# Encoder layer for two sequences: the split parts of ten weight chunks kept in DRAM by the first sequence and loaded by the second

## The chip, the core and the metric

One core of a Trainium2 chip runs the whole kernel in one launch. The metric is device time in microseconds (us); lower is better. TensorE (PE in the profile) does the matmuls, VectorE (DVE), ScalarE (ACT) and GpSimd (POOL) the rest; all transfers are issued by SyncE (SP), one after the other.

## What is computed

One encoder layer on two independent sequences of 512 rows with 1024 columns, float32 in and out. Cut to what matters here:

```python
h = rms_norm(x, pre_g)
z = h @ w_in                         # split into mixers, gates and merge gates
q = rms_norm(c_q, q_norm_g) @ w_uq   # 8 heads of 64 + 32 (rope) columns
kv = rms_norm(c_kv, kv_norm_g) @ w_ukv   # 8 heads: 64 columns of k, 64 of v
y_attn = attention(q, k, v) * silu(g_attn)
m = (gates[0] * (y_pool @ w_up_pool) + gates[1] * (y_attn @ w_up_attn)
     + gates[2] * (y_conv @ w_up_conv) + gates[3] * (y_four @ w_up_fourier))
out = x + rms_norm(m @ w_out, post_g)
```

Both sequences use the same weights: `w_uq` (chunks of kind h), the k and v columns of `w_ukv` (kinds kn and v) and the four `w_up` matrices (kind u) are the ones that count below.

## The kernel before

**Split matmuls.** A float32 operand is held as two fp32r parts, a rounded one (hi) and the rest (lo = source - hi). `mm3` (L569) makes a product of three matmuls: hi x hi, hi x lo, lo x hi. `split` (L574) makes the parts: an ACT copy writes hi, then a subtraction writes lo. The subtraction is recorded by `either`, so it may run on DVE or on POOL.

**Weight chunks.** A unit of work (`_Unit`) names the chunks that it needs by a key (sequence, kind, number). Line 619 sets the sequence to 0 for kinds that both sequences share, and for u chunks 0 to 5, which are used by both sequences in one stage; so these are loaded and split once. The chunks h 0 and 1 (128x768), kn 0 and 1 (128x256), v 0 and 1 (128x256) and u 6 to 9 (128x1024, the attention branch's up projection) carry the sequence's own number: they are loaded and split once for each sequence. `acquire` (L1632) does it: `load` (L1635) issues a DMA of the raw chunk, `into` (L1641) allocates the two parts and calls `split`.

**The order of the work.** Every call is recorded as an atom by `_Recorder`, and its `emit` (L182) writes all instructions, so nearly every row of the profile shows L182. `plan` (L285) is a list scheduler: it has one queue each for PE, ACT, DVE, POOL and the DMAs, prices for every operation (`price`, L184; a DMA costs `DMA_START` and its bytes over `DMA_RATE`, L113), due times that run back from PE's order, and a limit of buffers (42 of 2048 columns, 16 of 512). It picks at each step the atom that can start first, by due time, and for `either` the engine that would end first. What comes out is a fixed order for each engine. An instruction at the head of an engine's queue that waits holds all behind it. This is so for SP too: a DMA that stores a tile waits in SP's queue until the tile is written, and the DMAs behind it wait with it.

**The stages that matter.** After the group products of the input projection (until about 560 us) comes the tail, in which PE's order weaves two things: the up projections with their merges (u chunks), first the three branches that both sequences do together, then the attention branch of the first, then of the second sequence; and each sequence's attention. For a sequence, `c_units` (L745) fetches its projected rows cn from DRAM (four DMAs, `cn`, L756), mixes the rotated columns and transposes them on PE; `v_units`, `k_unit` and `q_unit` (L795 to L865) multiply them with v, kn and h chunks; each of the first two query blocks is put together by five or so DMAs from tile to tile (`b<-b` in the profile), the others are stored and fetched later. Then the heads follow.

Of the kernel before, what the change touches and what calls it, by code (L numbers as in the profile page):

```python
# [12 lines left out]
F32 = mybir.dt.float32  # L13
F32R = mybir.dt.float32r
# [4 lines left out]
P = 128  # L19
# [460 lines left out]
def trunk_kernel(ctx: ExitStack, tc: tile.TileContext, a: dict):  # L480
# [4 lines left out]
    rec = _Recorder()  # L485
# [9 lines left out]
    act, dve, pool, pe, sync = (Engine(e) for e in ("act", "dve", "pool", "pe", "dma"))  # L495

    def either(out, x, y, op):

        c = ("tensor_tensor", (out, x, y), dict(op=op))
        rec.choice(dve=c, pool=c)  # L500

    def copied(out, x):
        rec.choice(act=("activation", (out, x, AF.Copy), {}), dve=("tensor_copy", (out, x), {}))
# [6 lines left out]
    def g_(dt=F32, w=512):  # L510
        return rec.new("g", (P, w), dt)

    def b_(shape, dt=F32):
        return rec.new("b", [P] + list(shape), dt)

    def f_(w=D):
        return rec.new("f", (P, w), F32)
# [9 lines left out]
    def nm(s):  # L527
        uid[0] += 1
        return f"{s}_{uid[0]}"
# [14 lines left out]
    def stored(shape):  # L544
        n = nm("st")
        return rec.new("dram", shape, F32, dp.tile(list(shape), F32, tag=n, name=n))
# [27 lines left out]
    def split(hi, lo, src):  # L574
        act.activation(hi, src, AF.Copy)
        if src.buf.kind == "ps":
            dve.tensor_tensor(lo, src, hi.bitcast(F32), op=ALU.subtract)
        else:
            for c in ((slice(0, 1), slice(1, 2)) if lo.idx.ndim == 2 and lo.idx.size == D else (slice(None),)):
                either(lo[:, c], src[:, c], hi[:, c].bitcast(F32), ALU.subtract)  # L580
# [1051 lines left out]
    def acquire(key):  # L1632
        kind = key[1]

        def load(i):  # L1635
            src, w = srcs[i]
            r = f_(w)
            sync.dma_start(r, src)
            return r

        def into(src):  # L1641
            w = src.shape[1]
            t = b_([2, w], F32R) if w > 512 else rec.new("w" if w > 256 else "g", (P, 2, w), F32R)
            split(t[:, 0], t[:, 1], src)
            return t[:, 0], t[:, 1]
        if kind[0] == "l":
            m = R[LEFT[int(kind[1])]]
            return into(m[:, key[2], :])
        if kind in ("r1", "r2"):
            g = g_()  # L1650
            sync.dma_start(g, a["wo"][key[2] + 4 * (kind == "r2")][:, :512])
            return into(g)
        if kind == "r7":
            r1, r2 = [load(("o", key[2] + i)) for i in (0, 4)]
            s3 = g_()
            t1, t2, t4 = r1[:, :512], r1[:, 512:], r2[:, :512]
            either(s3, r2[:, 512:], t2, ALU.subtract)
            either(t1, t2, t1, ALU.subtract)
            either(t2, r2[:, 512:], t1, ALU.subtract)
            either(t4, t2, t4, ALU.subtract)  # L1660
            raws["o", key[2]] = {"r7": s3, "r5": t1, "r6": t2, "r4": t4, "r3": r2[:, 512:]}
        if kind[0] == "r":
            return into(raws["o", key[2]][kind])
        if key[1:] == ("q", 0):
            r, t = f_(832), b_([2, 832], F32R)
            for c in (slice(0, 416), slice(416, 832)):
                sync.dma_start(r[:, c], srcs["q", 0][0][:, c])
                copied(t[:, 0, c], r[:, c])
                dve.tensor_tensor(t[:, 1, c], r[:, c], t[:, 0, c].bitcast(F32), op=ALU.subtract)
            return t[:, 0], t[:, 1]  # L1670
        if kind == "q":
            r, t = load(key[1:]), b_([2, 832], F32R)
            copied(t[:, 0], r)
            either(t[:, 1], r, t[:, 0].bitcast(F32), ALU.subtract)
            return t[:, 0], t[:, 1]
        if kind[0] != "g":
            return into(load(key[1:]))
        if kind == "ga":
            r = raws[key[2]] = b_([2, 2, 512])
            for j, i in enumerate(PAIRS[key[2]]):  # L1680
                sync.dma_start(r[:, :, j, :], a["wt"][i].rearrange("p (h c) -> p h c", h=2))
            t = b_([2, 1024], F32R)
            split(*[t[:, i].rearrange("p (a b) -> p a b", a=2) for i in range(2)], r[:, :, 0, :])
            return t[:, 0], t[:, 1]
        r = raws[key[2]]
        r1a, r2a, r1b, r2b = [r[:, i, j, :] for i in range(2) for j in range(2)]
        if kind == "gb":
            s3 = raws["s3", key[2]] = g_()
            either(s3, r1a, r2a, ALU.subtract)
            either(r2a, r2a, r2b, ALU.add)  # L1690
            either(r1a, r2a, r1a, ALU.subtract)
        if kind == "gd":
            return into(raws["s3", key[2]])
        if kind == "gc":
            either(r1b, r1b, r1a, ALU.subtract)
        t = b_([2, 1024], F32R)
        split(*[t[:, i].rearrange("p (a b) -> p a b", a=2) for i in range(2)], r[:, int(kind == "gc")])
        return t[:, 0], t[:, 1]

    raws, owned = {}, set()  # L1700
    rec.unit()
    pool.memset(mhalf, -0.5)
    for n, u in enumerate(prog):
        if n == fixed:
            rec.floor = len(rec.segs)
        for k in u.chunks:
            if k not in owned:
                owned.add(k)
                rec.unit(0.0, None if n < fixed else PLAN["aheado" if k[1][0] in "lr" else "ahead"])
                live_chunks[k[1:]] = acquire(k)  # L1710
        rec.unit(u.cost, u.ahead if n >= fixed else None)
        u.fn()
# [124 lines left out]
```

## Time and profile before

| | us |
|---|---|
| median of 3 runs | 923.95 (922.61 to 928.17) |
| the profiled execution | 927.52 |
| its span on the core | 925.7 |
| PE busy | 898.8 (97%) |
| DVE, ACT, POOL busy | 721.9, 492.2, 359.4 |
| moved by DMA | 129.86 MB, 140 GB/s over the span |

The span runs from the first to the last record of the core; 1.8 us of the execution lie around it. The mean granted clock of TensorE was 0.997 of full speed. In the profile an operation is written as out<-in with the program's names, numbers left out: `ps` are PSUM tiles, `b` wide and `g` narrow SBUF tiles, `st` tiles in DRAM, `in_...` inputs in DRAM. "[0.5 <-DVE b]" behind a row says that the engine was idle for 0.5 us ahead of it, and that a DVE instruction on a `b` tile ended that.

### The profile page before, as it was taken

How to read it: one execution, taken by the hardware profiler on the slowest of the kernel's cores; microseconds unless marked ns; L12 is line 12 of the kernel's file. 1: busy time of each engine (PE TensorE's matmuls, PEld its weight loads, DVE VectorE, ACT ScalarE, POOL GpSimd, SP SyncE). 2: the span in 40 equal slices, each digit the busy share in tenths (PEclk: the TensorE clock that was granted, in tenths of full speed). 3: DMA queues.
4: the chain of work that ended last, by engine and by line, in shares of the span. 5: the costliest groups of instructions: out<-in, count | busy, mean ns of one | idle time of the engine just before them, and what ended most of it. 6: DMA issues, size and time to landing. Idle time of an engine off the chain costs nothing. (4 is left out here: it accounts for less than half of the span.)

```text
span 925.7 us, 12147 instructions
## 1 busy us (share of the span) xinstructions
PE 898.8 (97%) x4125; PEld 725.4 (78%) x4125; DVE 721.9 (78%) x1089; ACT 492.2 (53%) x871; POOL 359.4 (39%) x305
## 2 busy tenths in 40 slices
PE   7999999999999999999999999899999999999996
PEld 6897877888778888877888887787778777777784
DVE  6889999689994655667634367978899778899998
ACT  7964233345443345435444456855676678873253
POOL 2798432126331322346100031412353344246935
PEclk9999999999999999999999999999999999999998
DMA  7140123332232333543322447866754564461124
GB/s 273 64 152 10 58 103 125 129 110 103 91 125 106 128 133 130 173 142 118 136 104 102 141 141 179 254 217 198 233 186 133 161 242 148 155 231 58 37 101 182
DMA packets 62258, 129.86 MB, mean 140 GB/s; under 512 B 6890, under 2 KB 10483, under 8 KB 61684
## 3 DMA queue, kind: packets, MB, share of 16 engines
q1 hardware_dynamic: 62196, 129.09, 41.7%
q8 instruction: 32, 0.52, 0.2%
q14 instruction: 30, 0.25, 0.1%
HBM read 88.56 MB, written 37.36 MB: 136 GB/s over the span
## 5 line engine op out<-in xcount | busy, mean ns | idle before, releaser
L182 PE MATMUL ps<-b,b 128*128 128x512 f32 (+3 forms) x3428 | 808.1, 392 | 9.9 <-DVE b L182 4.7
L182 PEld LDWEIGHTS ps<-b,b 128*128 128x128 f32 (+1 forms) x3428 | 626.5, 187 | 158.0 <-DVE b L182 6.7
L182 ACT ACTIVATE b<-b 128x1024 fp32r<-128x1024 f32 (+9 forms) x164 | 141.3, 880 | 127.6 <-PE ps L182 46.4
L182 POOL TENSOR_TENSOR b<-b,b 128x512 fp32r<-128x512 f32 (+4 forms) x79 | 120.8, 1542 | 141.1 <-ACT b L182 134.5
L182 DVE TENSOR_TENSOR b<-b,b 128x512 fp32r<-128x512 f32 (+5 forms) x167 | 144.5, 892 | 31.6 <-ACT b L182 30.6
L182 POOL TENSOR_TENSOR b<-g,b 128x512 fp32r<-128x512 f32 x48 | 69.0, 1442 | 133.3 <-ACT b L182 133.3
L182 DVE TENSOR_TENSOR g<-ps,g 128x512 f32<-128x512 f32 (+4 forms) x101 | 66.2, 658 | 63.6 <-PE ps L182 35.8
L182 ACT ACTIVATE g<-ps 128x512 f32<-128x512 f32 (+5 forms) x110 | 59.4, 542 | 88.3 <-PE ps L182 71.9
L182 DVE TENSOR_TENSOR b<-ps,b 128x512 fp32r<-128x512 f32 (+2 forms) x128 | 85.0, 682 | 21.2 <-ACT b L182 20.4
L182 DVE SCALAR_TENSOR_TENSOR ps<-b,cols,ps 128x512 f32<-128x512 f32 x116 | 87.3, 752 | 2.7
L182 ACT ACTIVATE b<-g 128x512 fp32r<-128x512 f32 x101 | 61.5, 629 | 32.3 <-DVE g L182 18.5
L182 ACT ACTIVATE b<-ps 128x512 fp32r<-128x512 f32 (+2 forms) x116 | 66.5, 593 | 19.9 <-PE ps L182 19.2
L182 DVE TENSOR_TENSOR b<-b 128x512 f32<-128x512 f32 (+4 forms) x69 | 61.9, 898 | 9.0 <-POOL g L182 4.0
L182 ACT ACTIVATE g<-ps,s 128x512 f32<-128x512 f32 (+1 forms) x77 | 48.5, 639 | 23.8 <-DVE s L182 14.9
L182 ACT ACTIVATE g<-g,cols 128x512 f32<-128x512 f32 x48 | 34.6, 721 | 48.7 <-DVE g L182 48.3
L182 POOL TENSOR_TENSOR b<-b 128x512 f32<-128x512 f32 (+3 forms) x32 | 43.7, 1367 | 39.2 <-DVE b L182 16.2
L182 POOL TENSOR_TENSOR b<-b,g 128x512 f32<-128x512 f32 x26 | 37.2, 1436 | 51.1 <-DVE g L182 36.0
L182 DVE TENSOR_TENSOR b<-g,b 128x512 fp32r<-128x512 f32 x53 | 51.2, 980 | 4.6 <-ACT b L182 4.1
L182 PE MATMUL ps<-b 128*128 128x512 f32 (+1 forms) x216 | 52.1, 388 | 1.2 <-DVE b L182 1.2
L182 POOL TENSOR_TENSOR g<-b 128x512 f32<-128x512 f32 x15 | 20.1, 1342 | 80.5 <-DMA b<-in_wt 47.7
L182 DVE TENSOR_REDUCE s<-ps 128x1 f32<-128x512 f32 x64 | 43.4, 681 | 4.9 <-PE ps L182 4.5
L182 PEld LDWEIGHTS ps<-b 128*128 128x128 f32 x216 | 39.5, 188 | 9.7 <-issue 1.4
(74 smaller groups left out, 563.4 us busy)
## 6 DMA issues: line engine op xcount, KB each, us to landing
st<-g SPq DMA_DIRECT2D x104, 256.0 KB, 2.0
b<-in_wt SPq DMA_DIRECT2D x50, 512.0 KB, 4.7
g<-st SPq DMA_DIRECT2D x100, 256.0 KB, 3.4
b<-in_x SPq DMA_DIRECT2D x15, 512.0 KB, 4.5
b<-in_wup SPq DMA_DIRECT2D x14, 512.0 KB, 4.5
b<-st SPq DMA_DIRECT2D x4, 1024.0 KB, 6.8
b<-in_wo SPq DMA_DIRECT2D x8, 512.0 KB, 6.7
out_y<-b SPq DMA_DIRECT2D x16, 256.0 KB, 2.1
```

The lines of the kernel that those rows point to most:

```text
L182: getattr(engines[atom.eng], method)(*[real(x) for x in args], **{k: real(x) for k, x in kw.items()})
```

## The change

For the ten chunks h 0 and 1, kn 0 and 1, v 0 and 1 and u 6 to 9, the first sequence loads and splits as before and then issues two stores, of hi and of lo, to a DRAM tile of twice the chunk's width. The second sequence issues one load of that tile instead of the raw load, the ACT copy and the subtraction. `PLAN` and the prices are as they were; the scheduler makes a new order from the changed atoms. The number of PE instructions stays (4127 in the program); ACT has 13 fewer, DVE 11 fewer, POOL 4 more, SP 20 more.

```diff
@@ acquire
+        if kind in ("h", "kn", "v", "u") and key[0] + (kind == "u" and key[2] < 6) == 0:
+            got = into(load(key[1:]))
+            w = got[0].shape[1]
+            split_before[key[1:]] = stored((P, 2, w))
+            for i in range(2):
+                sync.dma_start(split_before[key[1:]][:, i, :], got[i].bitcast(F32))
+            return got
+        if key[1:] in split_before:
+            w = split_before[key[1:]].shape[2]
+            t = b_([2, w], F32R) if w > 512 else rec.new("w" if w > 256 else "g", (P, 2, w), F32R)
+            sync.dma_start(t.bitcast(F32), split_before[key[1:]])
+            return t[:, 0], t[:, 1]
         if kind[0] != "g":
             return into(load(key[1:]))
@@
-    raws, owned = {}, set()
+    raws, owned, split_before = {}, set(), {}
```

The instructions that go or change engine, counted over the whole program: ACT loses four copies of 128x1024, two of 128x768 and four of 128x256 (and three small ones go to DVE); of the subtractions 128x1024 DVE loses three and POOL one, of 128x768 DVE and POOL one each, of 128x256 POOL four. Besides, the scheduler gives POOL ten subtractions or additions of 128x512 that DVE had. On SP, ten raw loads become ten loads of twice their bytes, and twenty stores of a part each are new: 6.8 MB more written and 3.4 MB more read.

Three places show how the order moves. The first is SP's queue where the first sequence's first h chunk (`in_wh`, later the tile b_658 before and b_666 now) is loaded and cn is fetched (`b_663` before, `b_675` now, from st_74 to st_77). Before:

```order
L182 DMA st_173<-g_652_4267 128x512
L182 DMA g_654_4288<-st_133 128x512
L182 DMA st_174<-g_637_4156 128x512
L182 DMA b_658_4311<-in_wh 128x768
L182 DMA b_663_4357<-st_74 128x416
L182 DMA b_663_4357<-st_75 128x416
L182 DMA b_663_4357<-st_76 128x416
L182 DMA b_663_4357<-st_77 128x416
L182 DMA st_175<-g_664_4361 128x512
```
Now:

```order
L182 DMA st_173<-g_661_4277 128x512
L182 DMA st_174<-g_647_4166 128x512
L182 DMA b_666_4319<-in_wh 128x768
L182 DMA g_667_4322<-st_132 128x512
L182 DMA g_668_4331<-st_133 128x512
L182 DMA st_178<-b_671_4357 128x768 x2
L182 DMA b_675_4382<-st_74 128x416
L182 DMA b_675_4382<-st_75 128x416
L182 DMA b_675_4382<-st_76 128x416
L182 DMA b_675_4382<-st_77 128x416
```
The two stores of the chunk's parts, st_178, stand between the load and the fetches.

The second is PE's queue at the transposes of that cn (`ident,b_663` before, `ident,b_675` now); ps_671 before and ps_676 now is one block of a group product. Before:

```order
L182 MATMUL ps_642_4189<-b_266_892,b_659_4328 128x512
L182 MATMUL ps_666_4382<-ident,b_663_4357 128x128 x4
L182 MATMUL ps_668_4390<-ident,b_663_4357 128x128 x4
L182 MATMUL ps_670_4399<-ident,b_663_4357 128x128 x4
L182 MATMUL ps_671_4405<-b_143_285,b_653_4286 128x512
L182 MATMUL ps_671_4405<-b_145_291,b_653_4286 128x512
L182 MATMUL ps_671_4405<-b_143_285,b_653_4286 128x512 x2
L182 MATMUL ps_671_4405<-b_145_291,b_653_4286 128x512
L182 MATMUL ps_671_4405<-b_143_285,b_653_4286 128x512
L182 MATMUL ps_676_4424<-ident,b_663_4357 128x128 x4
```
Now:

```order
L182 MATMUL ps_652_4199<-b_276_902,b_669_4340 128x512
L182 MATMUL ps_676_4393<-b_153_295,b_662_4296 128x512
L182 MATMUL ps_676_4393<-b_155_301,b_662_4296 128x512
L182 MATMUL ps_676_4393<-b_153_295,b_662_4296 128x512 x2
L182 MATMUL ps_676_4393<-b_155_301,b_662_4296 128x512
L182 MATMUL ps_676_4393<-b_153_295,b_662_4296 128x512 x2
L182 MATMUL ps_676_4393<-b_155_301,b_662_4296 128x512
L182 MATMUL ps_676_4393<-b_153_295,b_662_4296 128x512 x2
L182 MATMUL ps_676_4393<-b_155_301,b_662_4296 128x512
L182 MATMUL ps_676_4393<-b_153_295,b_662_4296 128x512
L182 MATMUL ps_678_4412<-ident,b_675_4382 128x128 x4
L182 MATMUL ps_679_4420<-ident,b_675_4382 128x128 x4
```
The transposes, which stood ahead of this block of twelve matmuls, now stand behind it.

The third is SP's queue where the first sequence's second h chunk and first v chunk are loaded, and its first query block (b_690 before, b_699 now) is put together by copies from tile to tile. Before:

```order
L182 DMA st_175<-g_664_4361 128x512
L182 DMA st_176<-g_667_4388 128x512
L182 DMA b_674_4420<-in_wh 128x768
L182 DMA b_674_4420<-in_wv 128x256
L182 DMA g_682_4470<-st_146 128x512
L182 DMA g_684_4475<-st_149 128x512
L182 DMA b_690_4502<-b_687_4486 32x1024 x2
L182 DMA b_690_4502<-b_690_4502 64x1024
L182 DMA st_177<-g_689_4493 128x512
L182 DMA st_178<-g_692_4525 128x512
L182 DMA b_690_4502<-b_687_4486 32x1024 x2
```
Now:

```order
L182 DMA b_686_4455<-in_wh 128x768
L182 DMA st_179<-g_682_4433 128x512
L182 DMA b_686_4455<-in_wv 128x256
L182 DMA st_181<-b_692_4489 128x768
L182 DMA st_183<-g_696_4507 128x256
L182 DMA st_181<-b_692_4489 128x768
L182 DMA st_183<-g_696_4507 128x256
L182 DMA b_699_4520<-b_699_4520 64x1024
L182 DMA b_699_4520<-b_697_4509 32x1024 x2
L182 DMA g_701_4548<-st_146 128x512
L182 DMA st_180<-g_700_4534 128x512
L182 DMA b_699_4520<-b_697_4509 32x1024 x2
```
The stores of hi and lo of the two chunks (st_181 and st_183, two each, 1 MB together) now stand ahead of all the copies.

## Rows read from the trace of the kernel before

**Rows 1.** This is the page, part 1: TensorE (PE), PE's weight loads, VectorE (DVE), ScalarE (ACT) and GpSimd (POOL), each with its busy time, its share of the span and its instructions.

```profile
PE 898.8 (97%) x4125; PEld 725.4 (78%) x4125; DVE 721.9 (78%) x1089; ACT 492.2 (53%) x871; POOL 359.4 (39%) x305
```

**Rows 2.** This is the busy time of every engine in eight stretches that follow each other, from where the first weights concerned are used to the end of the span. Columns: the stretch and its length, then busy time and instructions of PE, PEld (weight loads), DVE, ACT and POOL, the granted clock of PE as a share of full speed, the mean busy share of the 16 DMA engines, and what they moved in GB/s.

```profile
515.00:562.00 47.00, 47.00 (x218) 38.46 (x217) 25.73 (x38) 22.61 (x37) 9.52 (x10) 1.00 0.45 143
562.00:600.00 38.00, 35.09 (x173) 27.68 (x172) 33.05 (x57) 30.75 (x63) 13.32 (x12) 1.00 0.81 227
600.00:639.00 39.00, 38.34 (x222) 31.75 (x221) 29.93 (x59) 22.33 (x44) 5.97 (x7) 1.00 0.63 208
639.00:706.00 67.00, 65.97 (x333) 52.41 (x332) 61.54 (x106) 47.34 (x93) 28.05 (x22) 1.00 0.64 209
706.00:765.00 59.00, 56.45 (x268) 42.84 (x267) 47.11 (x83) 40.15 (x79) 23.36 (x17) 1.00 0.53 170
765.00:793.00 28.00, 28.00 (x138) 22.20 (x137) 24.27 (x46) 22.43 (x48) 10.92 (x8) 1.00 0.35 117
793.00:830.00 37.00, 35.84 (x180) 28.44 (x179) 33.18 (x54) 29.62 (x59) 14.21 (x11) 1.00 0.68 234
830.00:925.70 95.70, 86.81 (x381) 69.53 (x379) 90.43 (x119) 40.55 (x85) 62.35 (x44) 0.97 0.27 94
```

**Rows 3.** This is what PE waited for between 515 and 830 us: time in total, number of waits, the longest.

```profile
PE ps L182 <- DVE b L182: 5.5, 9, 1.7
PE ps L182 <- ACT g L182: 1.2, 2, 0.6
```

**Rows 4.** This is a list of the instructions of 515 to 830 us in groups of one shape each: count, busy time and mean ns of one, and the engine's idle time ahead of them with what ended it.

```profile
L182 ACT ACTIVATE b<-b 128x1024 fp32r<-128x1024 f32 x19 | 20.1, 1059 | 10.5 <-PE ps L182 4.8 <-DMA b<-in_wt 2.2 <-DMA b<-in_wup 2.0
L182 ACT ACTIVATE b<-b 128x768 fp32r<-128x768 f32 x4 | 3.4, 842 | 2.7 <-PE ps L182 1.8 <-DMA b<-in_wh 1.0
L182 ACT ACTIVATE g<-b 128x256 fp32r<-128x256 f32 x8 | 3.3, 415 | 1.5 <-DMA b<-in_wk 1.5
L182 DVE TENSOR_TENSOR b<-b,b 128x1024 fp32r<-128x1024 f32 x11 | 13.9, 1261 | 3.2 <-ACT b L182 3.2
L182 POOL TENSOR_TENSOR b<-b,b 128x1024 fp32r<-128x1024 f32 x3 | 7.5, 2516 | 0.9 <-ACT b L182 0.9
L182 POOL TENSOR_TENSOR b<-b,b 128x768 fp32r<-128x768 f32 x2 | 3.7, 1856 | 4.5 <-ACT b L182 4.5
L182 POOL TENSOR_TENSOR g<-b,g 128x256 fp32r<-128x256 f32 x8 | 8.0, 994 | 47.3 <-ACT g L182 44.6 <-DMA b<-st 2.8
L182 DVE TENSOR_TENSOR b<-g,b 128x512 fp32r<-128x512 f32 x18 | 15.2, 855 | 1.5 <-ACT b L182 1.3
L182 POOL TENSOR_TENSOR b<-g,b 128x512 fp32r<-128x512 f32 x23 | 31.2, 1364 | 81.5 <-ACT b L182 81.5
```

**Rows 5.** This is the timeline about 594 us: start, time, engine and instruction, with the idle time ahead of it and what ended it.

```profile
593.76 2.35 POOL L182 TENSOR_TENSOR b<-b,b 128x1024 fp32r<-128x1024 f32 x1
594.34 1.80 DVE L182 COPY g<-g 128x2 f32<-128x2 f32 x1
596.87 1.41 PE L182 MATMUL ps<-b,b 128*128 128x512 f32 x5 [1.75 <-DVE b L182]
```

**Rows 6.** This is the timeline from 531 to 548 us (SPq are the DMAs that SyncE issues; `in_wh` is the first chunk of kind h, `b<-st` the four fetches of cn, `b<-b,b 128x768` the low part of the h chunk, `ident,b` the transposes of cn).

```profile
531.71 12.51 PE L182 MATMUL ps<-b,b 128*128 128x512 f32 x53
532.91 0.38 SPq L182 DMA_DIRECT2D b<-in_wh  x1
538.87 1.75 SPq L182 DMA_DIRECT2D b<-st  x4
540.04 0.95 DVE L182 TENSOR_TENSOR b<-b,b 128x768 fp32r<-128x768 f32 x1
544.06 1.47 PE L182 MATMUL ps<-ident,b 128*128 128x128 f32 x12
544.18 1.14 POOL L182 TENSOR_TENSOR b<-b,kcs 128x64 f32<-128x64 f32 x3 [5.34 <-DMA b<-st]
```

**Rows 7.** This is the timeline of SPq from 546 to 561 us, and PE at 563.84 (`in_wh` is the second h chunk, `b<-b` the copies that put a query block together).

```profile
546.01 0.63 SPq L182 DMA_DIRECT2D b<-in_wh  x1
555.99 1.90 SPq L182 DMA_DIRECT2D b<-b  x3
557.95 2.38 SPq L182 DMA_DIRECT2D st<-g  x2
560.71 1.16 SPq L182 DMA_DIRECT2D b<-b  x2
563.84 6.41 PE L182 MATMUL ps<-b,b 128*128 128x512 f32 x27 [0.53 <-DMA b<-b]
```

**Rows 8.** This is the timeline of ACT at 743 and 749 us, and of PE at 752 us.

```profile
743.32 1.06 ACT L182 ACTIVATE b<-b 128x1024 fp32r<-128x1024 f32 x1 [0.61 <-DMA b<-in_wup]
748.95 1.06 ACT L182 ACTIVATE b<-b 128x1024 fp32r<-128x1024 f32 x1 [1.42 <-DMA b<-in_wup]
752.38 1.42 PE L182 MATMUL ps<-b,b 128*128 128x512 f32 x5 [0.81 <-DVE b L182]
```

**Rows 9.** This is the view of group 2 for the stretch 732 to 750 us.

```profile
732.00:750.00 18.00, 16.56 (x79) 12.16 (x78) 13.07 (x24) 12.48 (x25) 7.74 (x6) 1.00 0.94 325
```

**Rows 10.** This is the list of DMA issues by form: their count, KB each, and the median time from issue to landing in us.

```profile
b<-in_wup SPq DMA_DIRECT2D x14, 512.0 KB, 4.5
b<-st SPq DMA_DIRECT2D x4, 1024.0 KB, 6.8
```

## The prediction

> **What bounds the kernel now.** I read the page's first part, then the busy time by stretches, PE's waits, the groups of instructions by shape, and last the timelines about the four places where the change adds something to SP's queue.
>
> PE is busy for 898.8 us, 97% of the span [rows 1]. The stretches show where the rest is [rows 2]: between 515 and 830 us, which holds every use of the ten chunks, PE is busy for 306.7 of 315 us (the sum of the first seven rows). So 8.3 us is all that a change which leaves the matmuls alone can win there. That is 0.9% of 923.95, just under the 1% (9.2 us) that a measurement of this kernel can tell from no change. The clock is 1.00 in all seven rows, so nothing is to be had from it either. The last stretch loses another 8.9 us, but the chunks play no part there. Of the 8.3 us, 5.5 are nine short waits for DVE writing `b` tiles and 1.2 are two waits for ACT [rows 3].
>
> **What it removes.** ACT loses 4 x 1.06 + 2 x 0.84 + 4 x 0.42 = 7.6 us of copies, POOL 2.52 + 1.86 + 4 x 0.99 = 8.4 us of subtractions, and DVE 3 x 1.26 [rows 4] + 0.95 [rows 6] = 4.7 us. These are splits of the second sequence, in 639 to 706 us (h, v, kn) and about 740 to 830 us (kn, u). In 639 to 706 PE is idle for 1.0 us, in 765 to 793 for none, in 793 to 830 for 1.2 [rows 2]: the splits lie beside matmuls. They are done long ahead of use: counted in the changed order, 135 PE instructions stand between the one that frees the buffer of the second kn's reload and its first use, 194 for the second h, 214 for u 6. Fifty-three matmuls take 12.5 us, or 0.24 each, and 12 transposes 1.5 us, or 0.12 each [rows 6], so 135 instructions are 16 to 32 us, against 6.8 us for a load of 1 MB [rows 10]. The reloads are not late, and the splits were not either.
>
> What can be won is indirect: DVE is busy for 254.8 of the 315 us (the same seven rows), and the ten 128x512 operations that go to POOL take 10 x 0.86 more from it [rows 4]. So DVE gets 4.7 + 8.6 = 13.3 us lighter, 5%. Its share of PE's waits, 5.5 us, is the bound of that gain; if the waits shrink as its load, or twice so, 0.3 to 0.6 us go. Against that stand the ten operations themselves: 1.36 us on POOL for 0.86 on DVE [rows 4], 0.5 us later each for whoever reads them, 5 us if PE waited for all of them. PE waits for few: nine times for DVE in 315 us. Range -5.5 to +5, taken at 0.
>
> Here POOL gets 10 x 1.36 - 8.4 = 5.2 us heavier, and beside a POOL subtraction of 2.35 us stands a DVE copy of two columns that took 1.80 us, after which PE stood for 1.75 [rows 5]. The Trainium skill ("SBUF — State Buffer", on the shared port pair) says that GpSimd and some VectorE instructions lock one pair of ports for their whole length and the loser stands still; this row agrees, and by that rule the ten moves would cost up to 10 x 1.36 us of DVE, where I take none, because fewer long subtractions (one 128x1024 and one 128x768 less on POOL) hold the ports.
>
> **What it adds at the first h chunk.** Now two stores stand in SP's queue between the load of `in_wh` and the four fetches of cn. The low part, the later of the two parts, was done at 540.04 + 0.95 = 540.99; the fetches were issued at 538.87 and took 0.44 each, and PE's transposes began at 544.06, just as POOL's first instruction on cn was released at 544.18 [rows 6]. With two stores of 0.44 behind 540.99 the fetches begin at 541.87, 3.0 us later, and cn lands at about 547.1. PE's order has twelve matmuls moved ahead of the transposes: 12 x 0.24 = 2.8 us, to 546.9. What is late next is cn, by 0.2 us; if the 0.8 MB stored ahead of it delay it at the 325 GB/s that the DMAs reached [rows 9], by 2.4 more. Range 0 to 2.6, taken at 0.5, since the DMA share in 515 to 562 is 0.45 [rows 2].
>
> **At the first query block.** Four stores (1 MB) stand ahead of all five copies. The second h chunk was requested at 546.01, and SP then stood until 555.99 [rows 7], so most of the wait for the low parts falls into a gap. An estimate: landed in 4.5 us like a load of 512 KB [rows 10], split in 0.84 + 1.86 us and followed by the v chunk's 0.99 on POOL [rows 4], they are ready at 554.2 at the earliest. The issues of the four stores, 0.5 us each, bring the first copy to between 555.99 and 558.0. The last two copies went at 560.71 because they stood behind stores that waited for other work [rows 7], and they still do. PE waited for them 0.53 us at 563.84. Cost -0.5 (that wait goes) to +1.8 + 3.2 (issues, and 1.05 MB at 325 GB/s all ahead of the copies) = +5; taken at +1.0, the middle of the 0 to 2.0 us by which the first copy starts later.
>
> **At u 6 to 9 of the first sequence.** Eight stores of 512 KB, 4.2 MB, come between 700 and 765 us. That stretch has a DMA share of 0.53 [rows 2], but 732 to 750 is full: 0.94 and 325 GB/s [rows 9]. Two loads land late there already: ACT, in order, stands for 0.61 and 1.42 us for `in_wup`, and PE soon for 0.81 [rows 8], 0.4 of ACT's 2.0. If one pair of stores, 1.05 MB or 3.2 us at 325 GB/s, goes ahead of each of the two loads, ACT waits 6.4 us more; if all stores find the free part of the stretch, none. I take half a pair, 1.6 us, of which PE gets 0.4: +0.6. The range is 0 to 6.4.
>
> The reloads of u (4 MB for 2 MB about 793 to 830, share 0.68 [rows 2]) have over 40 us until use: 0, at most the 1.2 us by which PE already waits there once more.
>
> **Sum.** 0 + 0.5 + 1.0 + 0.6 + 0 = +2.1 on the profiled execution of 927.52 us (its span 925.7 and 1.8 around it), so 929.6. That execution lies 0.4% above the median of the runs; on the median 923.95 the same is **926.0 us**, within 1%.
>
> **Rivals.**
>
> *PE's gaps close (a gain).* If a lighter DVE and ACT end PE's waits for them, 5.5 + 1.2 us go [rows 3] and the three places cost nothing: 923.95 - 6.7 = 917.3; about half of it, 920.5, is likelier. For it speaks that DVE ends most of the waits; against it that 3.6 of the 8.3 us lie in 562 to 639 us [rows 2], where no split goes. Still within 1%; only all 8.3 us and something in the last stretch would make more.
>
> *The stores crowd 732 to 750 us (slower).* The stretch has no room: 4.2 MB at 325 GB/s are 12.9 us of all DMA engines, and behind them in SP's queue stand the loads of u 8 and 9, query blocks and gates. If three of the four pairs, 9.7 us, get ahead of loads that ACT stands for, and PE gets all of it because the attention's work behind them on ACT is late too, it is 923.95 + 9.7 and the first two places' 1.5, or 935.1. It decides from the point where loads of 512 KB land in 8 us or more there, instead of 4.5 [rows 10]. For it speaks the 0.94; against it that the order places the stores apart, and that the 1 MB fetch of a query block behind them is used some 20 us after it lands. The Trainium skill ("DMA: Bandwidth & Descriptors", "Issuing engines are not separate DMA queues") says that all transfers run on the same 16 engines and interleave, so a store takes its time from the loads beside it; the full stretch agrees with it, and by it this rival holds wherever the two overlap.
>
> *The change does not do what it says.* The order shows ten reloads and ten splits fewer; I give it nothing.
>
> **How the numbers follow.** The forecast, a few small costs: 0.58, with its own range 923 to 930. The gain: 0.19, of which 0.03 faster than 1%. The crowded stretch: 0.23, of which 0.17 beyond 1%, the rest a milder form. Together faster 0.03, same 0.80, slower 0.17. The range reaches into both rivals, 918.5 to 935.
>
> **What would show it.** Right: PE's busy time about 899 us; ACT 7.6 us less; PE's wait at the transposes of cn under 1 us, at the first query block 0.5 to 2 us, ACT's wait for `in_wup` under 4 us. Wrong: a PE wait of over 3 us at any of the three places, loads of u landing in 8 us or more, or PE's idle time between 515 and 830 under 4 us.

## The result and the profile after

The changed kernel takes 937.15 us (median of 4 runs, 932.86 to 939.5) where the kernel before takes 925.63 (4 runs, 922.61 to 928.17): a ratio of 1.0114, 95% interval 1.0088 to 1.0139. It is slower by about 1.1%: the medians lie 11.5 us apart, and 1.14% of 925.63 is 10.6 us. The forecast was 926.0, a loss of 2.1 us, with a range up to 935.0.

The profiled execution took 939.5 us, the longest of the four, with a span of 937.7: 12.0 more than before. This is part 1 of its page:

```profile
PE 902.0 (96%) x4125; PEld 728.3 (78%) x4125; DVE 712.6 (76%) x1078; ACT 486.1 (52%) x858; POOL 365.5 (39%) x309
```

The instructions changed about as predicted: PE does the same number, DVE is busy for 9.3 us less than in [rows 1] (13.3 were reckoned), ACT for 6.1 less (7.6), POOL for 6.1 more (5.2). The time went elsewhere. This is the busy time by stretches, columns as in [rows 2]:

```profile
515.00:562.00 47.00, 46.47 (x214) 37.67 (x213) 24.61 (x38) 21.65 (x34) 12.17 (x12) 1.00 0.52 171
562.00:600.00 38.00, 33.40 (x149) 26.83 (x149) 26.77 (x47) 28.30 (x56) 10.34 (x10) 0.91 0.79 218
600.00:639.00 39.00, 36.88 (x208) 30.90 (x208) 30.53 (x57) 20.86 (x43) 9.61 (x9) 0.96 0.62 204
639.00:706.00 67.00, 66.14 (x337) 52.24 (x337) 61.41 (x105) 44.56 (x86) 22.27 (x18) 1.00 0.73 232
706.00:765.00 59.00, 55.03 (x266) 43.19 (x265) 48.59 (x88) 38.25 (x76) 17.88 (x14) 1.00 0.70 221
765.00:793.00 28.00, 26.23 (x131) 20.51 (x130) 23.23 (x40) 21.35 (x44) 10.48 (x9) 1.00 0.63 205
793.00:830.00 37.00, 37.00 (x184) 29.43 (x183) 26.65 (x54) 27.80 (x59) 10.07 (x8) 1.00 0.54 198
830.00:937.70 107.70, 95.12 (x418) 75.20 (x417) 94.36 (x121) 46.09 (x95) 79.86 (x57) 0.97 0.33 118
```

Between 515 and 830 us (the first seven rows) PE is busy for 301.15 us, where it was busy for 306.69 before [rows 2]: it stands still for 13.85 us instead of 8.31, or 5.5 more. After 830 it is busy for 95.12 us instead of 86.81. So 8.3 us of its work have moved past 830; what the 5.5 us of waits don't account for, some 3 us, is an estimate of what the lower clock took. The rest of the 12.0 us is lost after 830. Against [rows 2], PE lost most in 562 to 639 and in 765 to 793, and its clock, 1.00 in all seven stretches before, was 0.91 and 0.96 in two of them. These are PE's waits in the same 315 us, to be read beside [rows 3]:

```profile
PE ps L182 <- DVE b L182: 8.5, 8, 2.7
PE ps L182 <- DVE g L182: 3.2, 2, 2.9
PE ps L182 <- DMA b<-b: 1.9, 1, 1.9
PE ps L182 <- DMA b<-st: 0.2, 1, 0.2
```

The first row of [rows 3] had nine waits and 5.5 us; now it has eight and 8.5, and two waits for a DVE `g` tile make another 3.2 (2.88 and 0.33). Three places hold most of them, and one more lies after 830 us.

**The first chunks, 545 to 565 us.** PE, SP and PE again, beside [rows 6, 7] (`st<-b` and `st<-g` are the stores of the parts of the second h and the first v chunk):

```profile
546.38 1.20 PE L182 MATMUL ps<-ident,b 128*128 128x128 f32 x9 [0.20 <-DMA b<-st]
553.68 0.32 SPq L182 DMA_DIRECT2D st<-b  x1
555.40 0.32 SPq L182 DMA_DIRECT2D st<-g  x1
555.82 0.38 SPq L182 DMA_DIRECT2D st<-b  x1
556.31 0.38 SPq L182 DMA_DIRECT2D st<-g  x1
557.27 1.86 SPq L182 DMA_DIRECT2D b<-b  x3
560.58 1.16 SPq L182 DMA_DIRECT2D b<-b  x2
565.04 1.17 PE L182 MATMUL ps<-b,b 128*128 128x512 f32 x4 [1.89 <-DMA b<-b]
```

PE stood for 0.20 us for cn, and for 1.89 us instead of 0.53 for the query block. The copies of that block started at 557.27 instead of 555.99, behind the four stores. But PE waited for the last two copies, and SP issued these from 560.58, no later than before (560.71 in [rows 7]): both times they were released as another copy of the block landed. What came later is their own landing. The run of the new order by itself, below, has this wait without the price of the stores.

**The later query blocks, 580 to 610 us.** SP, ACT, POOL, DVE and PE, in order of time:

```profile
577.64 1.73 POOL L182 TENSOR_TENSOR g<-b,g 128x256 fp32r<-128x256 f32 x1 [0.62 <-ACT g L182]
577.93 0.37 SPq L182 DMA_DIRECT2D st<-g  x1
579.39 0.34 SPq L182 DMA_DIRECT2D st<-g  x1
581.82 4.47 SPq L182 DMA_DIRECT2D st<-b  x6
588.73 1.07 ACT L182 ACTIVATE b<-ps 128x512 fp32r<-128x512 f32 x2 [3.25 <-DMA st<-b]
590.10 3.87 PE L182 MATMUL ps<-b,b 128*128 128x512 f32 x9 [2.71 <-DVE b L182]
599.88 2.35 POOL L182 TENSOR_TENSOR b<-b,b 128x1024 fp32r<-128x1024 f32 x1
599.93 2.33 DVE L182 COPY g<-g 128x2 f32<-128x2 f32 x1
602.99 1.46 PE L182 MATMUL ps<-b,b 128*128 128x512 f32 x4 [2.12 <-DVE b L182]
```

Among the stores of the later query blocks (`st<-b` here) stand those of the second v chunk (`st<-g` at 577.93 and 579.39); the one of the low part waited until POOL had written it, at 579.37. The query blocks' stores land later, and at 588.73 ACT has waited 3.25 us to write a buffer that one of them still reads ("[3.25 <-DMA st<-b]" in the row). DVE waits for ACT, and PE for DVE: 2.71 us. The kernel before has no such wait here. Then the granted clock falls. These are stretches around that wait, and four more that are spoken of below:

```profile
585.00:590.00 5.00, 2.39 (x13) 1.75 (x11) 1.92 (x5) 1.75 (x5) 0.00 (x0) 1.00 0.88 224
590.00:595.00 5.00, 4.90 (x18) 4.03 (x19) 4.11 (x8) 4.97 (x11) 2.55 (x2) 0.66 0.74 185
591.00:592.00 1.00, 1.00 (x4) 0.72 (x4) 0.96 (x3) 1.00 (x3) 0.56 (x1) 0.50 0.91 193
604.00:607.00 3.00, 3.00 (x10) 2.34 (x9) 3.00 (x8) 0.80 (x3) 1.43 (x2) 0.50 0.37 133
566.00:570.00 4.00, 4.00 (x12) 3.09 (x12) 3.04 (x6) 2.80 (x7) 0.00 (x0) 0.57 0.88 190
758.00:766.00 8.00, 7.38 (x38) 6.09 (x39) 7.35 (x13) 6.21 (x12) 3.32 (x2) 1.00 1.00 333
```

Behind the wait the granted clock was 0.66 on average over 5 us, and 0.50 in 591 to 592: the lower of the two levels, 1.2 GHz. The nine matmuls of the row at 590.10 took 3.87 us, 0.43 each instead of 0.24, or 1.7 us more in all. The wait at 602.99 is that of [rows 5], a DVE copy of two columns beside a long POOL subtraction, now 2.33 and 2.12 us. The clock was at 0.50 after it too, in 604 to 607, and it had fallen for the first time behind the wait of 1.89 us at 565.04 (0.57 in 566 to 570). Behind the longest wait of all, 2.88 us at 758.62 (below), it stayed at 1.00: the length of a wait alone does not tell whether the clock falls.

**The u chunks, 739 to 759 us.** To be read beside [rows 8]:

```profile
739.00 8.67 SPq L182 DMA_DIRECT2D st<-b  x12
747.77 0.61 SPq L182 DMA_DIRECT2D b<-in_wup  x1
753.40 1.06 ACT L182 ACTIVATE b<-b 128x1024 fp32r<-128x1024 f32 x1 [2.96 <-DMA b<-in_wup]
758.62 0.73 PE L182 MATMUL ps<-b,b 128*128 128x512 f32 x2 [2.88 <-DVE g L182]
```

SP issued twelve stores in a row in 8.67 us, with the two of u 7 among them; the load of u 8 followed at 747.77, landed when ACT began its copy at 753.40, and held ACT for 2.96 us, and PE for 2.88. In the kernel before ACT stood twice for this, 0.61 and 1.42 us, and PE for 0.81 [rows 8]. So ACT's wait grew by 0.9 us in all, and PE's by 2.1. Two more waits of PE, 1.19 and 0.58 us at 777 and 781, make the loss in 765 to 793; ahead of the first, ACT had stood for 1.15 us at 772.32 for a load of `in_wo`.

**The out stage, after 830 us.** Groups of the instructions after 830 us, before and then after (columns as in [rows 4]):

```profile
L182 POOL TENSOR_TENSOR b<-b,b 128x512 fp32r<-128x512 f32 x11 | 17.2, 1580 | 6.3 <-ACT b L182 6.3
L182 DVE TENSOR_TENSOR b<-b,b 128x512 fp32r<-128x512 f32 x25 | 20.4, 862 | 0.5 <-ACT b L182 0.3
```

```profile
L182 POOL TENSOR_TENSOR b<-b,b 128x512 fp32r<-128x512 f32 x16 | 25.6, 1613 | 8.4 <-PE ps L182 5.9 <-ACT b L182 2.4
L182 DVE TENSOR_TENSOR b<-b,b 128x512 fp32r<-128x512 f32 x20 | 23.9, 1236 | 1.2 <-ACT b L182 1.2
```

POOL has five more of these subtractions and DVE five fewer, but DVE's took 1.24 us each instead of 0.86. In the trace it is those that run beside a POOL operation that are long: 14 of the 20, at 1.47 us on average, while the other six took 0.68; before it was 10 of 25, at 1.13, and 0.68 for the rest. PE waited 2.4 us in this stage where it had no wait before, and between the last matmul and the end of the span lie 10.2 us instead of 8.8. That is 3.8 of the 12.0 us, and the runs with the old engines below tell which part goes with the assignment.

### The profile page after: what moved, and what is told of

Its sections match the earlier page's. It is cut to its first block, busy times and chain, and to the rows that moved or that the text cites. A ratio compares the mean times of both kernels' runs of the same rounds, so it can differ in the third digit from the quotient of the medians.

```text
span 937.7 us, 12183 instructions
## 1 busy us (share of the span) xinstructions
PE 902.0 (96%) x4125; PEld 728.3 (78%) x4125; DVE 712.6 (76%) x1078; ACT 486.1 (52%) x858; POOL 365.5 (39%) x309
## 4 chain that ended last, share of the span: by engine, by line
PE 63%; DVE 15%; POOL 6%; DMA 5%; issue 4%; ACT 4%; SPq 1%; DVEq 0%; POOLq 0%; ACTq 0%
PE ps L182 63%; DVE b L182 7%; DVE ps L182 4%; POOL b L182 4%; DVE g L182 3%; ACT b L182 2%; DMA b<-b 1%; POOL g L182 1%; ACT g L182 1%; SPq L182 1%; DVE s L182 1%; DMA g<-st 1%; DMA st<-g 1%; POOL s L182 1%; DMA g<-in_wo 1%
## 5 line engine op out<-in xcount | busy, mean ns | idle before, releaser
L182 PE MATMUL ps<-b,b 128*128 128x512 f32 (+3 forms) x3500 | 827.3, 393 | 15.6 <-DVE b L182 8.7
L182 PEld LDWEIGHTS ps<-b,b 128*128 128x128 f32 x3500 | 642.9, 188 | 165.0 <-DVE b L182 8.7
L182 ACT ACTIVATE b<-b 128x1024 fp32r<-128x1024 f32 (+7 forms) x156 | 135.3, 883 | 127.3 <-PE ps L182 49.4
L182 POOL TENSOR_TENSOR b<-b,b 128x512 fp32r<-128x512 f32 (+3 forms) x86 | 129.8, 1522 | 142.0 <-ACT b L182 129.3
L182 POOL TENSOR_TENSOR b<-g,b 128x512 fp32r<-128x512 f32 x42 | 60.4, 1441 | 121.8 <-ACT b L182 104.6
L182 POOL TENSOR_TENSOR b<-b,g 128x512 f32<-128x512 f32 x33 | 48.2, 1467 | 64.8 <-DVE g L182 52.9
L182 DVE TENSOR_TENSOR b<-g,b 128x512 fp32r<-128x512 f32 x59 | 54.0, 931 | 6.0 <-ACT b L182 5.1
L182 PE MATMUL ps<-ident,g 128*128 128x128 f32 (+1 forms) x281 | 43.2, 275 | 4.9 <-DMA g<-in_pre 2.6
L182 POOL TENSOR_TENSOR b<-b 128x512 f32<-128x512 f32 (+3 forms) x29 | 37.7, 1300 | 25.4 <-DVE b L182 13.5
L182 ACT ACTIVATE g<-g,s 128x512 f32<-128x512 f32 x54 | 38.9, 722 | 15.6 <-DVE s L182 15.3
```

The source lines that it names most:

```text
L182: getattr(engines[atom.eng], method)(*[real(x) for x in args], **{k: real(x) for k, x in kw.items()})
```

## The experiments

Three kinds of kernels follow: some are planned anew, some keep the order of the kernel before (the "old order") or of the changed kernel, and only the named DMAs are added or replaced when the program is written out. A ratio is to the kernel before on the same chip, with its 95% interval; the medians of before were 925.1 to 927.8.

### Which chunks cost

```diff
-        if kind in ("h", "kn", "v", "u") and key[0] + (kind == "u" and key[2] < 6) == 0:
+        if kind == "u" and key[0] + (kind == "u" and key[2] < 6) == 0:
```

> Only u 6 to 9 are stored and loaded as parts; h, kn and v are split twice as before. Theory A (stores at the head of SyncE's queue hold the transfers behind them, and so ACT and PE): the two losses between 545 and 625 us go, the one at about 755 us stays (a PE wait of 2 to 3 us), so 927 to 930 us. Theory B (the cost is the new assignment of operations to VectorE and GpSimd that the planner makes, whatever is stored): the out stage still has some 55 GpSimd instructions after 830 us instead of 44, and 929 to 933 us. Rival (the extra megabytes on the DMA engines): u is 8.4 of the 10.2 MB, so most of the loss stays, 934 us or more.

931.58 us, ratio 1.0051 (1.0028 to 1.0074). The waits between 545 and 625 went, as theory A has it, but so did the one at about 755: PE's longest wait there was 1.27 us. POOL had 51 instructions after 830 us, near the 55 of theory B, and PE waited 3.4 us there. The profiled execution, 927.12 us, is one of the three shortest of ten; six took 931.5 to 932.9, and what these lost more is not shown.

```diff
+        if kind in ("h", "kn", "v") and key[0] + (kind == "u" and key[2] < 6) == 0:
```

> Only h, kn and v are stored and loaded as parts; u 6 to 9 are split twice as before. Theory A: the losses between 545 and 625 us stay (PE waits of about 2 us for the query copies and 2.7 us for ACT behind a store, and a lower clock after it), the one at 755 us goes: 931 to 935 us. Theory B: depends on the new assignment alone, the sum with the run that does u only need not be that of the whole change. Rival (megabytes): 1.8 of 10.2 MB, so 926 to 928 us.

933.73 us, ratio 1.0067 (1.0046 to 1.0088). The copies of the query block held PE for 1.61 us and the place at 586 for 1.75, much as in the whole change. Not as expected, ACT still waited 5.4 us for `in_wup`, with no store of a u chunk in the queue; PE's next wait, at 752, was 1.43. The bytes in the two expectations are wrong: the DMAs moved 6.29 MB more with u alone and 3.93 MB more with h, kn and v alone (136.15 and 133.79 MB against 129.86), so the small chunks are 38% of the added bytes. They cost about as much as u; a cost that went by the bytes alone, 0.73% for u and 0.45% for the small chunks, lies at the very edge of both intervals. The two losses together, 1.0118, are about the whole change's 1.0114.

### The assignment of operations

```diff
     def choice(self, **alts):
+        e = next(self.WAS)      # the engine's first letter, 800 of them, from the kernel before
+        alts = {k: v for k, v in alts.items() if k[0] == e}
```

> The whole change, but each operation that may run on either of two engines is given the engine that it had in the kernel before (82 of 800 differ); the order is planned anew. Theory A: the losses at 545 to 625 and at 755 us stay, only the 3 to 4 us of the out stage may go: 932 to 936 us. Theory B: most of the loss goes: 926 to 930 us.

934.81 us, ratio 1.0076 (1.0049 to 1.0103). Most of the loss stays, so theory B is not the main cause. 0.4 points may belong to the assignment, but this interval and that of the whole change overlap. Not as expected, PE's waits after 830 us did not go: they are 2.6 us, so they belong to the new order and not to the assignment. What went is the end: 7.9 us lie behind the last matmul, where it was 10.2 in the changed kernel and 8.8 before.

### The old order

```diff
             a = rec.atoms[n]
+            if a in again:      # where the second sequence's ACT copy stood
+                nc.sync.dma_start(both_parts, stored_parts)
+            if a in skip:       # its raw load and its split
+                continue
             rec.emit(a, engines, tile_of)
+            if writes_a_part(a):    # of the first sequence's ten chunks
+                nc.sync.dma_start(stored_part, part)
```

> The whole change in the order of the kernel before: the ten raw loads and splits of the second sequence are left out, their reloads are issued where the ACT copy stood, and the stores right behind the instruction that writes each part; nothing else moves and no operation changes engine. Theory A: the stores still stand in SyncE's queue ahead of the query copies, the stores of later query blocks and the loads of u: 929 to 935 us, with PE waits at about 563, 580 to 590 and 750 us. Theory B: 924 to 927 us. Rival (megabytes): as the changed kernel, 935 us or more.

943.5 us, ratio 1.0169 (1.0132 to 1.0207). That is beyond theory A's 935 and where the rival has it. No operation changed engine or place, and the loss is larger than the whole change's: stores and reloads cost without any new order, and more in the old one. Whether it is the places in the queue or the megabytes, this run does not tell.

### Stores alone and reloads alone

The stores alone are the second half of that edit:

```diff
+            if writes_a_part(a):
+                nc.sync.dma_start(stored_part, part)
```

> The kernel before in its own order, with only the twenty stores added, each right behind the instruction that writes the part; the second sequence still loads the raw chunks and splits them. Theory A (the stores' places in SyncE's queue are the whole cost): as the run with stores and reloads in the old order, 939 to 945 us, with the PE waits at about 544, 566, 591 to 600 and 750 to 770 us. Rival (the reloads, 3.4 MB more to read, carry a good part of it): 930 to 937 us.

941.93 us, ratio 1.0164 (1.0135 to 1.0193). The stores alone make the whole loss of the old order. The largest wait, ACT and then PE, in order of time:

```profile
757.66 1.06 ACT L182 ACTIVATE b<-b 128x1024 fp32r<-128x1024 f32 x1 [2.69 <-DMA b<-in_wup]
769.83 0.63 ACT L182 ACTIVATE b<-g 128x512 fp32r<-128x512 f32 x1 [5.50 <-DMA g<-in_wo]
771.72 1.12 PE L182 MATMUL ps<-ident,g 128*128 128x128 f32 x4 [5.50 <-DVE b L182]
```

SP, held by the stores of u 8 and 9, issued a load of `in_wo` for the out stage at 762.86, it landed 6.9 us later, and ACT, in order, waited 5.50 us for it. PE got all of that.

The reloads alone are its first half, with another source:

```diff
+            if a in again:
+                nc.sync.dma_start(both_parts, one_stored_pair[:, :, :w])
+            if a in skip:
+                continue
```

> The order of the kernel before without the twenty stores: one 1 MB pair of parts of another weight is stored once at about 300 us, and the second sequence loads all its ten chunks from that (so it computes with other weights) and splits none of them. Theory A: the removed splits were beside the path and the reloads come in time: 923 to 928 us, no PE wait over 2 us that the kernel before does not have. Rival (the doubled reloads hurt): 929 us or more. Rival (the splits were worth something): under 922 us.

926.12 us, ratio 0.9996 (0.9982 to 1.0009). Ten splits gone and ten reloads of twice the bytes: no difference beyond 0.2%. PE's waits from 515 to 830 us:

```profile
PE ps L182 <- DVE b L182: 4.4, 6, 1.6
PE ps L182 <- ACT g L182: 1.3, 2, 0.8
```

They are those of [rows 3] less 1.1 us. The saving that the change aims at and the cost of the reloads together are 0, as forecast.

### The hold in the queue, or the bytes

Each store writes one partition of its part instead of 128 (it waits for the same instruction), or all 128 from `qcs`, a table that is ready from the start (the same bytes, no wait for a part).

```diff
-                nc.sync.dma_start(dst[:, i, :], got[i])
+                nc.sync.dma_start(dst[:1, i, :], got[i][:1])
```

> Order of the kernel before with the twenty stores behind the splits, as in the run with stores only, but each stores one partition of its part (4 KB or less) instead of 128: SyncE waits for the same instructions, the bytes are gone, and the raw chunks are split by the second sequence as before. If the hold in SyncE's queue is the cost: 936 to 942 us. If the transfer of 6.8 MB beside other transfers is: 925 to 929 us.

934.02 us, ratio 1.0071 (1.0040 to 1.0101). PE's waits, 515 to 830 us:

```profile
PE ps L182 <- DVE b L182: 8.1, 8, 2.0
PE ps L182 <- DMA b<-st: 2.0, 2, 1.8
```

```diff
-                nc.sync.dma_start(dst[:, i, :], got[i])
+                nc.sync.dma_start(dst[:, i, :], qcs[:, :dst.shape[2]])
```

> The same, with full size: each store writes as many bytes at the same place, but from a table that lies in SBUF from the start, so that it waits for no split. If the hold is the cost: 925 to 930 us. If the transfer is: 936 to 942 us. If each is half of it: both runs about 931 to 935 us.

935.34 us, ratio 1.0105 (1.0076 to 1.0134). The same view:

```profile
PE ps L182 <- DVE b L182: 11.4, 9, 2.9
PE ps L182 <- ACT g L182: 1.3, 2, 0.7
```

Neither theory is right alone: both times lie between the two expectations, near the 931 to 935 us of half each. The run with the hold costs 0.71% and the one with the bytes 1.05%, together 1.76% beside the 1.64% measured for both. Each of the two also has the twenty issues themselves; what these cost in the old order was not measured. The profiles separate them by place. With the hold alone PE waited 1.79 us for cn at 545, the term "at the first h chunk"; with the bytes alone it did not, but PE stood for 2.77 and 2.86 us at 748 and 765, behind ACT, whose rows there name transfers that landed late (`g<-st` and `in_wo`).

The same two in the order of the changed kernel, at the place where its stores are written out:

```diff
+            if stores_a_part(a):
+                nc.sync.dma_start(dst, qcs[:, :dst.shape[1]])
+                continue
```

> The changed kernel in its own order, with the twenty stores taken from the ready table (the second sequence then loads the table's numbers as its parts): the same bytes at the same places, without the waits for hi and lo. Hold: 928 to 931 us, that is what is left is the new assignment of operations. Transfer: 934 to 938 us, with the PE waits at about 587 and 757 us still there.

934.85 us, ratio 1.0098 (1.0073 to 1.0124). The waits at about 588 (2.14 us) and 752 (2.53) stayed, as expected for the transfer, and so did the 1.78 us for the query block.

```diff
+            if stores_a_part(a):
+                nc.sync.dma_start(dst[:1], src[:1])
+                continue
+            if loads_parts(a):
+                nc.sync.dma_start(dst, table_in_dram[:, :, :w])
+                continue
```

> The changed kernel in its own order, with stores of one partition each (and the second sequence's loads taken from a 1 MB table stored once at about 300 us): the waits for the parts stay, the bytes of the stores go. Hold: 934 to 938 us. Transfer: 928 to 931 us, with no PE wait over 2 us at 587 and 757 us and the 3 to 4 us of the out stage left.

932.91 us, ratio 1.0076 (1.0050 to 1.0102). The wait at about 755 is down to 0.90 us (at 758), that at 588 to 1.66, and the one for the query block is 1.77; the time lies between the two expectations.

### The new order by itself

Both edits at once: one ready partition is stored, and the second sequence loads from a table.

```diff
-                nc.sync.dma_start(dst[:1], src[:1])
+                nc.sync.dma_start(dst[:1], qcs[:1, :dst.shape[1]])
```

> The changed kernel in its own order with neither price of the stores: each stores one partition of a table that is ready from the start, and the second sequence's loads come from a 1 MB table stored once at about 300 us. If the new order by itself costs nothing, 924 to 927 us, and the hold and the transfer then make the whole loss and overlap in it; if the new assignment of operations and the new order cost by themselves, 929 to 932 us, and that part is in every run of the changed order.

933.03 us, ratio 1.0049 (1.0031 to 1.0067). PE's waits from 515 to 830 us:

```profile
PE ps L182 <- DVE b L182: 6.5, 9, 1.9
PE ps L182 <- DMA b<-b: 1.8, 1, 1.8
```

The new order costs 0.5% without either price of the stores. PE still waits 1.8 us for the query block, though SP has issued the four small stores 3.9 us ahead of the first copy, and 1.65 and 1.95 us at about 589 and 601. These waits are thus the new order's, but others went for them: between 515 and 830 us PE is as busy as before, 306.20 us beside 306.69. The loss lies behind (the stretches as in [rows 2]):

```profile
515.00:830.00 315.00, 306.20 (x1524) 244.56 (x1523) 246.97 (x435) 207.29 (x403) 94.61 (x79) 1.00 0.62 195
830.00:931.20 101.20, 87.76 (x382) 69.01 (x380) 89.64 (x111) 42.18 (x86) 76.97 (x54) 0.96 0.28 102
```

From 830 us to the end it is 101.2 us instead of 95.7 [rows 2], about the whole loss: 3.4 us of waits of PE, 10.0 us instead of 8.8 behind the last matmul, and 1.0 us more of matmuls.

With this and the edit of `choice` above, planned anew:

> As the run before it, planned with the engine that each operation had in the kernel before. If the loss of the new order is the assignment to VectorE and GpSimd: 924 to 927 us. If it is the order itself, about the same as the run before it, within 1 us.

930.54 us, ratio 1.0033 (1.0015 to 1.0051). The two intervals overlap, but they share their uncertain base, the kernel before on that chip. The times themselves do not overlap: ten executions took 929.2 to 931.8 us, and the four of the run before it 932.7 to 933.1. So the old engines are worth some 2.5 us here, and the 2.8 us that are left go with the order. The profiles agree: PE still waits 2.6 us after 830, but 7.8 us instead of 10.0 lie behind the last matmul.

### Stores moved away

In the old order:

```diff
-            if writes_a_part(a):
-                nc.sync.dma_start(stored_part, part)
+            for b in last:
+                if last[b] == n:      # the last matmul that reads the chunk
+                    for i in range(2):
+                        nc.sync.dma_start(dst[:, i, :], got[i])
```

> The whole change in the order of the kernel before, but both stores of a chunk are issued right behind the first sequence's last matmul that reads it, instead of behind its split. Theory A: no store then waits for a low part in front of other transfers, but the stores of h, kn and v 1 still stand among the copies and stores of the query blocks at 563 to 590 us and those of u 6 to 9 no longer stand ahead of the loads of u 8 and 9: 928 to 933 us. Rival (the megabytes themselves): 938 us or more, as with the early stores.

931.95 us, ratio 1.0058 (1.0036 to 1.0080): a third of the loss of the old order is left. One place is as long as all of it:

```profile
585.55 1.41 SPq L1766 DMA_DIRECT2D st<-g  x2
590.80 0.63 ACT L182 ACTIVATE g<-g 128x512 f32<-128x512 f32 x1 [6.59 <-DMA st<-g]
592.81 0.58 PE L182 MATMUL ps<-g,g 128*128 128x256 f32 x1 [5.69 <-DVE g L182]
```

A store at a chunk's last use holds the chunk's buffer: ACT wanted the `g` tile next and waited 6.59 us for the store to land, PE 5.69.

```diff
+        for k in u.chunks:
+            if k in pending and final[k] == n:      # the last unit that uses the chunk
+                rec.unit()
+                got = pending.pop(k)
+                for i in range(2):
+                    sync.dma_start(split_before[k[1:]][:, i, :], got[i].bitcast(F32))
```

> The changed kernel, with the stores of a chunk recorded behind the unit that uses it last, so that the planner orders everything with late stores. Theory A: the waits at about 563, 587 and 755 us shrink, the out stage may still pay for more GpSimd operations: 927 to 933 us. Rival (megabytes, or the planner's new assignment): 934 us or more.

932.65 us, ratio 1.0067 (1.0043 to 1.0092). Better than the change, still slower than before. Since the reloads in place of the splits are worth nothing (at most 0.2%), a better placing of the stores can save their price, but there is nothing to win beyond that.

## Why the prediction was wrong

The runs add up in points of a per cent (the two middle rows of the old order keep the second sequence's splits, which the reloads alone show to be worth nothing):

| | old order | changed order |
|---|---|---|
| reloads, stores free | -0.04 | +0.49 |
| with the hold alone | +0.71 | +0.76 |
| with the bytes alone | +1.05 | +0.98 |
| with both | +1.69 | +1.14 |

- **What it removes: 0.** Right: 0.9996 with the splits gone. PE's gaps could not be closed by a lighter DVE or ACT.
- **The reloads: 0.** Right, by the same run.
- **At the first h chunk: +0.5.** Right in the changed order (0.20 us; the twelve matmuls cover it). In the old order, where they do not, PE's longest wait for cn is 1.54 us with the stores alone and 1.79 with the hold alone.
- **At the first query block: +1.0.** The number came (1.89 - 0.53 = +1.4), but by luck. The text read the last two copies of [rows 7] as held by stores and let the four new stores move the copies; in the trace the two are released by the landing of another copy, at the same time as before, and PE waits 1.8 us for them in the changed order even with no price of the stores. It is the new order's wait. Which transfer beside them makes them land later was not tested. (In the old order the stores do make a wait there, 1.04 us; the hold alone or the bytes alone make none.)
- **At u 6 to 9: +0.6.** This step failed. I let ACT wait 1.6 us more and PE have 0.4 of it, the ratio of [rows 8]. ACT waited only 0.9 us more in all, but in one piece of 2.96 us, and PE had 2.88 of it: its wait grew by 2.1 us. The ratio of one place is no rate for another: 5.50 of 5.50 us reached PE in the run with stores alone, about 1.4 of 5.4 with h, kn and v alone. By the runs in the changed order it is the bytes that make this wait (2.53 us with the bytes alone, 0.90 with the hold alone).
- **The places.** This step failed too. The text counted three places at which stores stand in SP's queue; the second v chunk, whose stores stand among those of the later query blocks, was a fourth, with the dearest wait between 545 and 625 us: 2.71 us, and the lower clock after it. I looked for loads that come late and not for buffers that come free late because a store from them does. Not all of it is the stores': 1.65 us are there in the changed order without their price.
- **The clock.** The text took from 1.00 in all seven rows that nothing was to be had from it, and not that it could be lost. It fell behind three waits, and by the estimate above that took some 3 us.
- **Ten operations to POOL: taken at 0, and the last stretch left out.** This is the largest term that is missing: 3.8 of the 12.0 us. The text said that the chunks play no part after 830 us; the planner's new order does. PE's 2.4 us of waits there stay when every operation has its old engine (2.6 us), so they are the order's; of the end behind the last matmul, 10.2 us, some 2.3 go with the new assignment. Ten was the net count: 82 of 800 operations changed engine. The lengthening that [rows 5] shows for one DVE copy beside POOL is there, 1.47 us for 0.68, but PE's waits there are as long with the old engines.
- **The crowded stretch** was the rival that came nearest, with 935.1, in part by luck: its 9.7 us at the u chunks were 2.1. Its mechanism holds (the bytes alone cost 1.05% in the old order), but not its condition: the page's loads of `in_wup` landed in a median of 4.4 us, and the one that ACT waited for in 5.6, not 8. It was enough that it was issued late, took 5.6 us to land where the load that ACT waited for at 743 us before [rows 8] took 4.0, and that ACT, in order, could do nothing else.

So the sum of +2.1 us was too small by 8 to 9: one share too low (u), one place left out, with the clock that fell, and the out stage, which the new order slowed. The signs that the text named for being right nearly all came (waits of 0.20, 1.89 and 2.96 us, none of PE over 3 us), because they watched the three places alone.

## What to carry to other kernels

A store that only saves later work is not free because nobody waits for it: its cost is what stands behind it, in the issuing queue while its source is unfinished, on the DMA engines while it moves, and in the buffer until it lands. Here the three show apart: 0.71% with the wait and without the bytes, 1.05% with the bytes and without the wait, and 6.59 us of ACT where a buffer was held. Before doing work once instead of twice, ask whether the second time was on the path: here ten splits and ten loads were worth 0.0%, and sparing them cost 1.1%. How much of an in-order engine's wait reaches the next depends on what lies ready there; a ratio measured at one place says little on another. And a scheduler that plans anew changes stages that the edit does not touch: a loss of half a per cent was there with stores of 4 KB or less that waited for nothing.

## What the runs showed of the hardware

- After a wait of 2.71 us PE's granted clock was 0.66 on average over 5 us (0.50, 1.2 GHz, in 591 to 592), and nine matmuls took 0.43 us each instead of 0.24: 1.7 us on top of the wait. It was at 0.50 behind waits of 1.89 and 2.12 us as well, but stayed at 1.00 behind one of 2.88 us, and in the run of the new order by itself behind waits of 1.82, 1.65 and 1.95.
- DMA issues took SP 0.44 us each in a group of four [rows 6], and 0.72 in the run of twelve (8.67 us); in the kernel before it was 0.63 in the run of ten at the same place (6.29 us). A long run of issues costs its issuer time too.
- DVE subtractions of 128x512 between SBUF tiles took 0.86 us on average with eleven of that form on POOL in the same stretch, and 1.24 with sixteen: 0.68 where no POOL operation ran beside them, 1.13 and 1.47 on average where one did.
